# Products of the modulation grouped by four with rows turned by transposes, and sample states loaded one half ahead, in a two-layer hybrid decoder step

## The chip, the cores and the metric

The kernel runs on one core of a Trainium2 chip. The metric is the time of one launch on the device in microseconds (us), as the median of three runs. The core has five engines that work side by side, each through its own queue in order: PE (TensorE, matmuls; its weight loads are listed apart as PEld), DVE (VectorE), ACT (ScalarE), POOL (GpSimd) and SP (SyncE, which here issues most of the loads from device memory). On-chip data lies in SBUF; PE writes to PSUM, from which DVE and ACT read.

## What is computed

Two consecutive layers of a decoder, for one prompt of 512 tokens and eight sample sequences of four tokens each, which share the weights. The kernel keeps all 544 tokens as columns and the 1024 features as rows in eight tiles of 128. The two places that matter here:

```
mod = (jax.nn.silu(c) @ lw['w_ada'] + lw['b_ada'])[:, None, :]
sh1, sc1, g1, sh2, sc2, g2 = jnp.split(mod, 6, axis=-1)
h = _rmsnorm(x, lw['norm1']) * (1 + sc1) + sh1
...
def step(h, inp):
    s, d = inp
    return h * d[..., None, None] + s, h
...
y_off = jnp.einsum('bclgn,bcgrpn->bclgrp', Cm, prev) * jnp.exp(cs)[..., None]
```

The first is the modulation: nine conditioning vectors (one of the prompt, eight of the samples) times a weight of 1024 by 6144, once per layer. The second is the state-space branch: for each of eight samples and four head groups an old state of 128 by 512 is multiplied by C (the product `y_off`), decayed, added to, and written back.

## The kernel before

All large projections go through `gemm` (L325): a tile of weights (128 by 1024, 512 KB) is loaded by SP into one of four `raw` buffers, split by ACT (`wh`) and DVE (`wl`) into a high and a low part with three buffers each (`weights`, L313), and multiplied in 48 matmuls of 272 columns: eight tiles of features, three products each (high by high, high by low, low by high), two halves of the columns. Every `gemm` first calls `pump` (L136), which takes a few steps from side programs. These are Python generators in lanes; each `yield` ends a step. So the side work is laid between the gemms, step by step. A list scheduler then fixes the order of the instructions on each engine from the order of the code, priorities, its own estimate of when inputs are there, and free buffers; `high_priority(offset=WPRI)` lets weight loads run ahead. Tiles of tag "T" (49 buffers) hold most intermediates, the state tiles `h0` among them.

**The modulation** (`ada`, L235) is one side program per third of a layer's weight. Its weight comes in 16 tiles of 512 KB (`raw<-w_ada`). A tile holds two slices of the contraction; each is multiplied by `self.sc` (L253), the activated conditioning vectors padded to 32 columns, so a product takes 128 by 32 by 512 and fills 32 rows of a PSUM tile. The slice number decides which of the four row groups (0, 32, 64, 96) it goes to, so that eight slices end as four partial sums in four row groups. Between the tiles stands a `yield`. ACT copies the 128 by 512 result into `adarow`; then four matmuls (L261) with the constant `s4`, in which every 32nd row has a one in the same column, turn a 128 by 128 piece and add its four row groups. DVE adds the bias into `mod` (L262). One such block of four tiles is gone through four times per third of a layer: 24 blocks and 192 products in all. The first third of layer 0 runs at the start, before any gemm, because the first norm needs it; the others run beside the pooling branch of layer 0 and, for layer 1, beside the FFN of layer 0.

**The sample part of the state branch** (`ssd_sample`, L1028) runs once per head group and layer, eight times in all, in two halves of four samples. Per half POOL spreads B over the samples (`bbd`, L1079), SP loads four old states `h0` (L1084), a `yield` follows, then four products of 128 by 32 by 512 (L1088), one per sample and row group, into `qp`; after another `yield` there are per sample a matmul of the new input (`up`, L1100), the decay on POOL (L1103), the sum on DVE (L1106), and the store of the new state.

Of the kernel before, what the change touches and what calls it, by code (L numbers as in the profile page):

```python
# [17 lines left out]
try:  # L18
# [5 lines left out]
F32 = mybir.dt.float32  # L24
# [4 lines left out]
OP = mybir.AluOpType  # L29
AX = mybir.AxisListType  # L30
# [16 lines left out]
WPRI = 300  # L47
# [51 lines left out]
C_ID, C_CAUS, C_TRI, C_BLK, C_TRIS, C_BLKS, C_SEL, C_RW, C_HM, C_SC, C_BM, C_NM, C_RC, C_S2, C_S4 = (  # L99
    0, 128, 256, 384, 386, 418, 450, 482, 738, 746, 810, 818, 822, 886, 950)  # L100
# [3 lines left out]
class Prog:  # L104
# [130 lines left out]
    def ada(self, l, s, first=False):  # L235

        nc, a = self.nc, self.a
        par, mod, _ = self.par[l]
        m0 = 16 * s
        pick = lambda x: x.rearrange("p (h c t) n -> p c h t n", h=2, c=4)  # L240
        dst = pick(mod[:, m0:m0 + 16, :])
        bias = par[:, P_BADA + m0:P_BADA + m0 + 16].rearrange("p (h c t) -> p c h t", h=2, c=4)
        s4 = self.c[:, C_S4:C_S4 + 32]
        for c in range(4):
            ps = self.P("ada1")
            for z in range(4):
                i = 4 * c + z
                with self.tc.high_priority(offset=WPRI):
                    raw = self.wr.tile([128, 1024], F32, name="raw", tag="raw")
                    nc.sync.dma_start(raw, a["w_ada"][l, s, i])  # L250
                for q in range(2):
                    k, g = 2 * z + q, 32 * (2 * (z % 2) + q)
                    nc.tensor.matmul(ps[g:g + 32, :], self.sc[:, k, :], raw[:, q * 512:(q + 1) * 512],  # L253
                                     start=(k < 4), stop=(k >= 4))
                if z < 3:
                    yield
            row = self.t("adarow")
            self.copy("ada2", row[:, :512], ps)
            ps2 = self.P("ada2" if first else "ada3")
            for b in range(4):  # L260
                nc.tensor.matmul(ps2[:, b * 32:(b + 1) * 32], row[:, b * 128:(b + 1) * 128], s4, start=True, stop=True)  # L261
            self.E("ada1").tensor_tensor(dst[:, c], ps2[:, :128].rearrange("p (h t n) -> p h t n", h=2, t=2)[:, :, :, :9],  # L262
                                    bias[:, c, :, :, None].to_broadcast([128, 2, 2, 9]), op=OP.add)
            yield

# [762 lines left out]
    def ssd_sample(self, q):  # L1028
        nc, a, l, c = self.nc, self.a, self.l, self.c
        par = self.par[l][0]  # L1030
        csr = self.csT.bitcast(F32R)
        g, cb, Cc, xss = q["g"], q["cb"], q["C"], q["xss"]
        ps = self.P("ssd_sample1")
        for jj in range(4):
            nc.tensor.transpose(ps[:32, jj * 128:(jj + 1) * 128], xss[:, jj, :], self.ident)
# [11 lines left out]
        ps = self.P("ssd_sample2")  # L1047
# [16 lines left out]
        for jj in range(4):  # L1064
            for e in range(2):
                i = 2 * jj + e
# [8 lines left out]
        for hf in range(2):  # L1075
            bbd = self.t("bbd")
            bm = c[:32, C_BM + 4 * hf:C_BM + 4 * hf + 4, None].to_broadcast([32, 4, 128])
            for r, src in enumerate((q["bh"], q["bh"], q["bl"])):
                self.E("ssd_sample7").tensor_tensor(  # L1079
                    bbd.bitcast(F32R)[32 * r:32 * r + 32, :512].rearrange("p (b n) -> p b n", b=4),  # L1080
                    src[:, None, :].to_broadcast([32, 4, 128]), bm, op=OP.mult)
            h0s = [self.t("h0") for z in range(4)]
            for z in range(4):
                nc.sync.dma_start(h0s[z][:, :512], a["h0"][l, g, 4 * hf + z])  # L1084
            yield
            for z in range(4):
                b = 4 * hf + z
                nc.tensor.matmul(qp[32 * z:32 * z + 32, :], cm[:, 32 * b:32 * b + 32], h0s[z][:, :512],  # L1088
                                 start=(hf == 0), stop=(hf == 1))
            if hf:  # L1090
                yq = self.t("yq")
                self.copy("ssd_sample18", yq[:, :512], qp)
                for jj in range(4):
                    nc.tensor.matmul(ys[:, 128 + jj * 32:160 + jj * 32], yq[:, jj * 128:(jj + 1) * 128],
                                     c[:, C_S4:C_S4 + 32], start=True, stop=True)
            yield
            for z in range(4):
                b = 4 * hf + z
                up = self.P("ssd_sample5")
                nc.tensor.matmul(up, bbd.bitcast(F32R)[:96, z * 128:z * 128 + 128], xr[:96, :512],  # L1100
                                 start=True, stop=True)
                hn = self.t("hn0")
                self.E("ssd_sample8").tensor_tensor(hn[:, :512].rearrange("p (h d) -> p h d", h=8),  # L1103
                                        h0s[z][:, :512].rearrange("p (h d) -> p h d", h=8),
                                        self.sdec[:, b, hs, None].to_broadcast([128, 8, 64]), op=OP.mult)
                self.E("ssd_sample9").tensor_tensor(hn[:, :512], hn[:, :512], up, op=OP.add)  # L1106
                nc.scalar.dma_start(a["o_ssds"][l, g, b], hn[:, :512])
                yield
# [3 lines left out]
                                op=OP.mult)  # L1112
# [656 lines left out]
```

## Time and profile before

| What | Value |
|---|---|
| Time, median of 3 runs | 3217.64 us (3216.38 to 3218.22) |
| Time of the profiled execution | 3219.4 us |
| Its span, first to last instruction | 3217.6 us |
| PE busy | 3117.6 us, 97% |
| DVE, ACT, POOL busy | 2229.4, 1258.1, 892.9 us |
| Mean granted TensorE clock | 0.985 |
| Products L253 (modulation), busy | 92.7 us, 384 records |
| Products L1088 (old states), busy | 44.5 us, 128 records |
| Folds L261 (modulation), busy | 24.5 us, 192 records |

A matmul of 32-bit floats shows as two records in the trace, one of the split type (`wh`, `wl` with `hh`, `hl`) and one transpose as one record. Matmuls overlap in the trace, since the next begins before the last has drained; what a matmul costs the engine is therefore read from the start of one to the start of the next, not from its listed duration.

### The profile page before, as it was taken

To read this page: it belongs to the slowest core of one execution; us is meant where nothing else is said; L and a number is where in the kernel's file an instruction comes from. 1 tells how busy PE (TensorE), PEld (TensorE's weight loads), DVE (VectorE), ACT (ScalarE), POOL (GpSimd) and SP (SyncE) were. 2 spreads that over 40 slices of the span, in tenths; PEclk is the share of its full clock that TensorE was granted. 3 is DMA by queue.
4 is the path that set the end of the run, shared out by engine and by line. 5 is a ranking of instruction groups with operands and counts; after the bars stand their busy time and mean duration, and the time that the engine had idled before them with its cause. 6 is when DMAs were issued, how large, how long until landed. Compare 5 with 4: busy or idle time off the path is not lost. (4 is left out here: it accounts for less than half of the span.)

```text
span 3217.6 us, 63012 instructions
## 1 busy us (share of the span) xinstructions
PE 3117.6 (97%) x24322; PEld 2834.3 (88%) x24322; DVE 2229.4 (69%) x4827; ACT 1258.1 (39%) x2228; POOL 892.9 (28%) x1271
## 2 busy tenths in 40 slices
PE   7999999999999999999999999999999999999999
PEld 5987898999896788888989978989999967899999
DVE  5687788679878655444566877886799976564554
ACT  4344443333236534333443444433342365352432
POOL 2373445421021002111223544455120210030211
PEclk8999999999999999999999999999999999999999
DMA  6332332345433434445334323233233234333322
GB/s 231 104 104 77 110 95 101 105 151 179 164 117 129 157 133 115 147 146 147 105 104 122 98 82 106 89 96 119 95 129 117 91 125 154 106 84 94 78 98 78
DMA packets 303102, 376.85 MB, mean 117 GB/s; under 512 B 177362, under 2 KB 186930, under 8 KB 302802
## 3 DMA queue, kind: packets, MB, share of 16 engines
q1 hardware_dynamic: 116514, 315.94, 29.3%
q10 hardware_dynamic: 181216, 42.05, 6.4%
q0 software_dynamic: 5072, 14.83, 1.2%
q8 instruction: 192, 3.15, 0.4%
q14 instruction: 108, 0.88, 0.1%
HBM read 330.34 MB, written 33.79 MB: 113 GB/s over the span
## 5 line engine op out<-in xcount | busy, mean ns | idle before, releaser
L177 ACT ACTIVATE wh<-raw 128x1024 fp32r<-128x1024 f32 (+2 forms) x434 | 424.9, 980 | 1199.7 <-PE psg L336 909.6
L336 PE MATMUL psg<-hh,wh 128*128 128x272 f32 x4064 | 863.7, 292 | 7.8 <-ACT cacc L839 5.4
L336 PE MATMUL psg<-hl,wh 128*128 128x272 f32 x4064 | 856.0, 290 | 0.0
L336 PE MATMUL psg<-hh,wl 128*128 128x272 f32 x4064 | 853.6, 290 | 0.0
L322 DVE TENSOR_TENSOR wl<-raw,wh 128x1024 fp32r<-128x1024 f32 (+2 forms) x434 | 510.5, 1176 | 354.1 <-ACT wh L177 349.8
L336 PEld LDWEIGHTS psg<-hh,wh 128*128 128x128 f32 x4064 | 642.6, 189 | 61.9 <-issue 28.1
L336 PEld LDWEIGHTS psg<-hh,wl 128*128 128x128 f32 x4064 | 643.9, 189 | 17.1 <-issue 15.3
L336 PEld LDWEIGHTS psg<-hl,wh 128*128 128x128 f32 x4064 | 644.1, 189 | 15.9 <-issue 14.4
L841 POOL COPY sti<-cu 128x32 f32<-128x32 f32 x136 | 91.3, 672 | 588.9 <-ACT cu L177 588.6
L846 DVE SCALAR_TENSOR_TENSOR cacc<-cu,half,cacc 128x511 f32<-128x511 f32 x144 | 134.9, 937 | 6.8 <-ACT cacc L839 6.3
L336 PE MATMUL psg<-fh,wh 128*128 128x272 f32 x648 | 135.4, 291 | 2.6 <-DVE resid L460 2.6
L855 ACT ACTIVATE th<-cacc 128x544 f32<-128x544 f32 x92 | 60.5, 657 | 196.1 <-DVE cacc L849 187.5
L454 DVE SCALAR_TENSOR_TENSOR x<-psg,mod,x 128x272 f32<-128x272 f32 x64 | 32.0, 500 | 151.6 <-PE psg L336 142.6
L336 PE MATMUL psg<-fl,wh 128*128 128x272 f32 x648 | 133.7, 287 | 0.0
L336 PE MATMUL psg<-fh,wl 128*128 128x272 f32 x648 | 133.7, 288 | 0.0
L336 PEld LDWEIGHTS psg<-fh,wh 128*128 128x128 f32 x648 | 101.2, 188 | 14.3 <-issue 6.7
L336 PE MATMUL psg<-oh,wh 128*128 128x272 f32 x512 | 110.4, 294 | 0.0
L336 PE MATMUL psg<-ol,wh 128*128 128x272 f32 x512 | 109.5, 291 | 0.0
L336 PE MATMUL psg<-oh,wl 128*128 128x272 f32 x512 | 109.0, 292 | 0.0
L856 DVE SCALAR_TENSOR_TENSOR cacc<-th,cacc 128x544 f32<-128x544 f32 x92 | 71.3, 775 | 49.2 <-ACT th L855 49.0
L986 POOL TENSOR_TENSOR seg<-seg,cb 128x512 f32<-128x512 f32 x64 | 88.9, 1392 | 54.3 <-ACT seg L985 46.8
L336 PEld LDWEIGHTS psg<-fl,wh 128*128 128x128 f32 x648 | 101.7, 188 | 0.0
(469 smaller groups left out, 6232.4 us busy)
## 6 DMA issues: line engine op xcount, KB each, us to landing
raw<-wk SPq DMA_DIRECT2D x326, 512.0 KB, 3.5
raw<-w_ada SPq DMA_DIRECT2D x96, 512.0 KB, 3.5
h<-h SPq DMA_DIRECT2D x64, 256.0 KB, 3.8
raw<-wk SPq DMA_DIRECT2D x64, 256.0 KB, 2.8
o_ssds<-hn ACTq DMA_DIRECT2D x64, 256.0 KB, 2.2
raw<-wd SPq DMA_DIRECT2D x32, 448.0 KB, 3.4
kvr<-ckv SPq DMA_DIRECT2D x48, 256.0 KB, 3.6
kvw<-ckv SPq DMA_DIRECT2D x48, 256.0 KB, 4.0
```

The source lines that it names most:

```text
L177: self.nc.scalar.activation(out, src, AF.Copy)
L322: self.last_wl = self.E("weights1").tensor_tensor(wl[:, :n], raw[:, :n], wh[:, :n].bitcast(F32), op=OP.subtract).ins
L336: nc.tensor.matmul(o[:, c, :HC], w[:, k * 128:(k + 1) * 128], x[:, c * HC:(c + 1) * HC], start=(k == 0 and first), stop=(k == K - 1 and last))
L454: self.E("resid1").scalar_tensor_tensor(x[:, :HC], o[:, 0, :HC], g[:, 0:1], x[:, :HC], op0=OP.mult, op1=OP.add)
L841: self.E("conv1").tensor_copy(st[:, i, :, W - 1:], new)
L846: self.E("conv3").scalar_tensor_tensor(acc[:, s:512], u[:, :512 - s], wc, acc[:, s:512], op0=OP.mult, op1=OP.add)
L855: nc.scalar.activation(th, acc, AF.Tanh)
L856: self.E("silu21").scalar_tensor_tensor(acc, th, 1.0, acc, op0=OP.add, op1=OP.mult)
L986: self.E("ssd_chain5").tensor_tensor(d[:, :512], d[:, :512], cb[:, :512], op=OP.mult)
```

## The change

In `ada` the two tiles of a pair are loaded in two steps as before, but no product is issued until both are there; then four products go out one after the other, into the four row groups. The number of steps per block (four) stays. The fold by matmuls with `s4` becomes four transposes by the identity, each 128 by 128, which fill a whole PSUM tile; DVE then adds the four row groups with one reduction (`adat`), and the bias is added from there. In `ssd_sample` the four loads of the first half move to the start of the side program, those of the second half directly behind the products of the first, and the `yield` that stood between loads and products goes (two steps fewer per call).

```diff
         for c in range(4):
             ps = self.P("ada1")
-            for z in range(4):
-                i = 4 * c + z
-                with self.tc.high_priority(offset=WPRI):
-                    raw = self.wr.tile([128, 1024], F32, name="raw", tag="raw")
-                    nc.sync.dma_start(raw, a["w_ada"][l, s, i])
-                for q in range(2):
-                    k, g = 2 * z + q, 32 * (2 * (z % 2) + q)
-                    nc.tensor.matmul(ps[g:g + 32, :], self.sc[:, k, :], raw[:, q * 512:(q + 1) * 512],
-                                     start=(k < 4), stop=(k >= 4))
-                if z < 3:
+            for pair in range(2):
+                raws = []
+                for z in (2 * pair, 2 * pair + 1):
+                    with self.tc.high_priority(offset=WPRI):
+                        raw = self.wr.tile([128, 1024], F32, name="raw", tag="raw")
+                        nc.sync.dma_start(raw, a["w_ada"][l, s, 4 * c + z])
+                    raws.append(raw)
+                    if z % 2 == 0:
+                        yield
+
+                for k4 in range(4):
+                    nc.tensor.matmul(ps[32 * k4:32 * k4 + 32, :], self.sc[:, 4 * pair + k4, :],
+                                     raws[k4 // 2][:, (k4 % 2) * 512:(k4 % 2) * 512 + 512],
+                                     start=(pair == 0), stop=(pair == 1))
+                if pair == 0:
                     yield
             row = self.t("adarow")
             self.copy("ada2", row[:, :512], ps)
             ps2 = self.P("ada2" if first else "ada3")
             for b in range(4):
-                nc.tensor.matmul(ps2[:, b * 32:(b + 1) * 32], row[:, b * 128:(b + 1) * 128], s4, start=True, stop=True)
-            self.E("ada1").tensor_tensor(dst[:, c], ps2[:, :128].rearrange("p (h t n) -> p h t n", h=2, t=2)[:, :, :, :9],
+                nc.tensor.transpose(ps2[:, b * 128:(b + 1) * 128], row[:, b * 128:(b + 1) * 128], self.ident)
+
+            tot = self.s([128, 4, 9], "adat")
+            nc.vector.tensor_reduce(tot, ps2.rearrange("p (b g n) -> p b n g", b=4, g=4)[:, :, :9, :],
+                                    axis=AX.X, op=OP.add)
+            self.E("ada1").tensor_tensor(dst[:, c], tot.rearrange("p (h t) n -> p h t n", h=2),
                                     bias[:, c, :, :, None].to_broadcast([128, 2, 2, 9]), op=OP.add)
             yield
...
+        def states(hf):
+            h0s = [self.t("h0") for z in range(4)]
+            for z in range(4):
+                nc.sync.dma_start(h0s[z][:, :512], a["h0"][l, g, 4 * hf + z])
+            return h0s
+        nxt = states(0)
         ps = self.P("ssd_sample1")
...
-            h0s = [self.t("h0") for z in range(4)]
-            for z in range(4):
-                nc.sync.dma_start(h0s[z][:, :512], a["h0"][l, g, 4 * hf + z])
-            yield
+            h0s = nxt
             for z in range(4):
                 b = 4 * hf + z
                 nc.tensor.matmul(qp[32 * z:32 * z + 32, :], cm[:, 32 * b:32 * b + 32], h0s[z][:, :512],
                                  start=(hf == 0), stop=(hf == 1))
-            if hf:
+            if not hf:
+                nxt = states(1)
+            else:
                 yq = self.t("yq")
```

The diff alone doesn't tell what order the scheduler makes of it. Line numbers of the changed kernel lie some lines further down: L253 becomes L256, L261 becomes L265, L336 becomes L344, L1088 becomes L1100, L1100 becomes L1114, L1084 becomes L1045.

On PE, beside the pooling branch of layer 0, the order before has a pair of modulation products between two gemms (`psg` is a gemm's result, `raw` the modulation's weight tile, `sc` the conditioning vectors; x2 counts equal instructions in a row):

```order
L336 MATMUL psg<-hl,wh 128x272 x2
L336 MATMUL psg<-hh,wl 128x272 x2
L253 MATMUL psb<-raw,sc 32x512 x2
L336 MATMUL psg<-ph,wh 128x272 x2
L336 MATMUL psg<-pl,wh 128x272 x2
```

and the changed order, in the same part of the program, has four:

```order
L344 MATMUL psg<-hh,wl 128x272 x2
L256 MATMUL psb<-raw,sc 32x512 x4
L344 MATMUL psg<-ph,wh 128x272 x2
L344 MATMUL psg<-pl,wh 128x272 x2
```

Twice as many products now stand in one place, and the next gemm boundary has none.

On PE, in the sample part of the first head group of layer 0, the second half's products stood one by one between gemm matmuls before (`h_2731` to `h_2734` are that half's states, `cm` is C, `rel` belongs to the indexer):

```order
L1088 MATMUL psa<-h_2731,cm 32x512
L745 MATMUL psb<-rel,wsel 32x512
L336 MATMUL psg<-hh,wl 128x272 x2
L1088 MATMUL psa<-h_2732,cm 32x512
L336 MATMUL psg<-hh,wh 128x272 x2
L336 MATMUL psg<-hl,wh 128x272 x2
L336 MATMUL psg<-hh,wl 128x272
L1088 MATMUL psa<-h_2733,cm 32x512
```

Now the two halves stand close together, the second one as four in a row (`h_2492` to `h_2495` first half, `h_2631` to `h_2634` second half; `bbd` feeds the matmul of the new input, `kx` the indexer):

```order
L1100 MATMUL psa<-h_2492,cm 32x512
L1082 MATMUL psb<-smt,sxdt 64x32 x8
L1100 MATMUL psa<-h_2493,cm 32x512
L1100 MATMUL psa<-h_2494,cm 32x512
L1100 MATMUL psa<-h_2495,cm 32x512
L1114 MATMUL psb<-sxst,bbd 128x512
L748 MATMUL psa<-kx,qis 32x512 x4
L1100 MATMUL psa<-h_2631,cm 32x512
L1100 MATMUL psa<-h_2632,cm 32x512
L1100 MATMUL psa<-h_2633,cm 32x512
L1100 MATMUL psa<-h_2634,cm 32x512
```

The gemm matmuls that parted them have moved behind them, and the first matmul with `bbd` stands directly behind the first half's products.

On SP, for the same place, three weight loads lay between the first and the second half's states before:

```order
L318 DMA raw<-wk 128x1024 x2
L318 DMA raw<-wk 128x512
L1084 DMA h_2731<-h 128x512
L1084 DMA h_2732<-h 128x512
L1084 DMA h_2733<-h 128x512
L1084 DMA h_2734<-h 128x512
```

and now one, with reads of the page table (`pt`) behind it:

```order
L326 DMA raw<-wk 128x1024
L835 TENSOR_LOAD pt
L835 ISA x2
L835 TENSOR_LOAD pt
L835 ISA x2
L1045 DMA h_2631<-h 128x512
L1045 DMA h_2632<-h 128x512
```

The second half's loads stand behind one weight load instead of three.

## Rows read from the trace of the kernel before

**Rows 1.** The page's head and part 1: span; busy time, share, instructions of each engine.
```profile
span 3217.6 us, 63012 instructions
...
PE 3117.6 (97%) x24322; PEld 2834.3 (88%) x24322; DVE 2229.4 (69%) x4827; ACT 1258.1 (39%) x2228; POOL 892.9 (28%) x1271
```

**Rows 2.** Waits of PE: engine and line waited for, us in total, times, longest.
```profile
PE psa L424 <- DVE sqb L395: 14.1, 1, 14.1
PE psa L433 <- DVE rstdh L276: 10.8, 6, 3.8
PE psg L353 <- ACT hh L177: 9.0, 4, 2.5
PE psb L1100 <- DVE hn L1106: 6.3, 2, 3.4
```

**Rows 3.** Timeline of PE (start, duration, engine, line, tiles): a pair of modulation products.
```profile
660.80 0.42 PE L336 MATMUL psg<-ol,wh 128*128 128x272 f32 x2
661.06 0.41 PE L336 MATMUL psg<-oh,wl 128*128 128x272 f32 x2
661.40 1.05 PE L253 MATMUL psb<-raw,sc 128*32 128x512 f32 x4
662.38 0.52 PE L336 MATMUL psg<-oh,wh 128*128 128x272 f32 x2
```

**Rows 4.** Timeline of PE: four modulation products in a row.
```profile
717.43 0.41 PE L1213 MATMUL psg<-ph,wl 128*128 128x272 f32 x2
717.77 1.07 PE L253 MATMUL psb<-raw,sc 128*32 128x512 f32 x8
718.77 0.52 PE L1213 MATMUL psg<-ph,wh 128*128 128x272 f32 x2
```

**Rows 5.** Timeline of PE: one product of an old state alone.
```profile
227.90 0.28 PE L336 MATMUL psg<-hh,wl 128*128 128x272 f32 x1
228.12 1.04 PE L1088 MATMUL psa<-h,cm 128*32 128x512 f32 x2
229.09 0.39 PE L336 MATMUL psg<-hh,wl 128*128 128x272 f32 x1
```

**Rows 6.** Timeline of PE: the fold of a modulation block by four matmuls.
```profile
1550.73 0.29 PE L336 MATMUL psg<-hh,wl 128*128 128x272 f32 x1
1550.86 0.97 PE L261 MATMUL psb<-cst,adarow 128*128 128x32 f32 x8
1551.67 0.37 PE L336 MATMUL psg<-hh,wl 128*128 128x272 f32 x1
```

**Rows 7.** Timeline of PE: four transposes of 128 by 128.
```profile
452.31 0.41 PE L336 MATMUL psg<-hh,wl 128*128 128x272 f32 x2
452.56 0.60 PE L965 MATMUL psa<-cst,cacc 128*128 128x128 f32 x4
452.92 0.50 PE L336 MATMUL psg<-hh,wh 128*128 128x272 f32 x2
```

**Rows 8.** Windows view of 452.50 to 453.50 us (PEclk is the granted clock); all transposes of L965.
```profile
452.50:453.50 1.00, 1.00 (x10) 1.00 (x9) 1.00 (x6) 0.94 (x1) 1.00 (x1) 1.00 0.00 0
...
L965 PE MATMUL psa<-cst,cacc x128: 270/272/472, 147.3 to 2202.3; 128*128 128x128 f32 x128
```

**Rows 9.** Windows view of the first 60 us: busy PE, PEld, DVE, ACT, POOL; granted clock, DMA.
```profile
0.00:60.00 60.00, 40.04 (x204) 24.26 (x204) 28.64 (x91) 25.20 (x54) 14.72 (x45) 0.89 0.74 259
```

**Rows 10.** Groups of DVE: the bias sum and the two nearest reductions.
```profile
L1470 DVE TENSOR_REDUCE smx<-psg 128x1 f32<-128x512 f32 x16 | 11.0, 688 | 9.2 <-PE psg L1462 9.1
...
L262 DVE TENSOR_TENSOR mod<-psb,par 128x36 f32<-128x36 f32 x24 | 4.6, 190 | 35.6 <-PE psb L261 35.6
...
L1471 DVE TENSOR_REDUCE smx<-psg 64x1 f32<-64x4 f32 x16 | 2.3, 143 | 0.0
```

**Rows 11.** What the products of the old states (L1088) waited for, us and times.
```profile
  POOL cm L1072: 5.7, 4
  issue: 3.6, 18
```

**Rows 12.** Waits of SP's DMA queue, us in total, times, longest.
```profile
SPq L318 <- DVE wl L322: 1546.5, 316, 12.1
SPq L250 <- PE psb L253: 271.4, 61, 6.6
```

More of the change, by code (lines that the diff above doesn't have):

```diff
@@ L242, in ada @@
         bias = par[:, P_BADA + m0:P_BADA + m0 + 16].rearrange("p (h c t) -> p c h t", h=2, c=4)
-        s4 = self.c[:, C_S4:C_S4 + 32]
         for c in range(4):
             ps = self.P("ada1")
-            for z in range(4):
-                i = 4 * c + z
-                with self.tc.high_priority(offset=WPRI):
-                    raw = self.wr.tile([128, 1024], F32, name="raw", tag="raw")
-                    nc.sync.dma_start(raw, a["w_ada"][l, s, i])
-                for q in range(2):
-                    k, g = 2 * z + q, 32 * (2 * (z % 2) + q)
-                    nc.tensor.matmul(ps[g:g + 32, :], self.sc[:, k, :], raw[:, q * 512:(q + 1) * 512],
-                                     start=(k < 4), stop=(k >= 4))
-                if z < 3:
+            for pair in range(2):
[12 more added lines that the diff above has]
+                if pair == 0:
                     yield
```

## The prediction

> **What bounds the kernel now.** I read the page's head first: PE is busy 3117.6 us of a span of 3217.6 [rows 1], and no other engine comes near. The waits of PE say what the missing 100 us are: the longest is the wait of 14.1 us for the first norm at the start, the next are norms of later stages, 9 to 11 us each in sum, and a matmul of the sample part with 6.3 us [rows 2]. No wait on a load is among the four longest. So from about 60 us on, what PE has to issue sets the time, and the right question is what the change takes from PE's queue; what lies on DVE, ACT, POOL and SP counts only where PE would wait for it. The first 60 us differ: PE is busy 40.0 of them, at a mean granted clock of 0.89 between the two levels of 1.2 and 2.4 GHz, with the DMA engines busy 0.74 [rows 9].
>
> **What a piece costs PE.** Matmuls overlap, so I take the time from the start of one gemm row to the start of the next gemm row behind the piece, and subtract what the gemm matmuls themselves take: a row of two starts 0.25 us after the one before, 0.125 each [rows 3].
> A pair of modulation products: from 661.06 to 662.38 is 1.32, less two gemm matmuls, 1.07 us [rows 3].
> Four in a row (four row groups): 717.43 to 718.77 is 1.34, less 0.25, 1.09 us [rows 4]. So four cost what two cost; products of 32 rows each in different row groups run at the same time, and the kernel before already does this in a few places.
> One product of an old state alone: 227.90 to 229.09 is 1.19, less 0.125, 1.07 us [rows 5]. It has the same shape, so one costs as much as four.
> I call each such visit a slot, at 1.07 us. The sum is then a count of slots in the two orders.
>
> **The change, part by part.**
> *Modulation products.* The order before has 192 products in 80 runs; the first 32, in 9 runs, belong to the start. The other 71 runs hold 72 slots (one run of six has two). The changed order has 51 runs; 6 hold the first 32 products, and each of the other 45 is one slot, nearly all of them four products. 72 less 45 is 27 slots, 27 x 1.07 = 28.9 us.
> *Old states.* 64 products stood in 40 runs (30 of one, 6 of three, 4 of four), each one slot; now in 20 runs, of which two hold seven products, so 22 slots. 18 x 1.07 = 19.3 us. The load ahead hides no wait that the trace has: these products waited 5.7 us for POOL's `cm` and for no load among the listed reasons [rows 11]. The gain comes from the order alone: the scheduler took the second half's states for late and spread their products over the gemms; now it sees them early.
> *Fold.* The old one takes from 1550.73 to 1551.67, less 0.125, 0.81 us [rows 6]; four transposes of the same operands' size take from 452.31 to 452.92, less 0.25, 0.36 us [rows 7]. 20 of the 24 folds lie behind the start: 20 x 0.45 = 9.0 us.
> *The start.* Here 15 slots become 10 and four folds shorten, but PE idles a third of the time [rows 9], because norm, loads and products take turns. Ends: none of it counts, or all of it, 5 slots and 4 x 0.45, some 7 us; a loss of a few us if the loads of a pair arrive late. I take 2 us, near the lower end, since an idle engine gains little from less work.
> *DVE.* 24 reductions of 36 sums over 4 are new. No row has this shape; the nearest are 0.143 us for 64 by 4 elements and 0.688 us for 128 by 512 [rows 10]. With 144 elements per row I put it at 0.3 us, nearer the small one; 7 us in all on an engine that is busy 69% [rows 1], and the last reader, `mod`, is due a whole stage later except at the start, where 4 x 0.3 is inside the 2 us taken. Cover gone, it would cost 24 x 0.69 = 17 us at most. The bias sum stays at 0.19 us.
> *Loads.* Their number and size stay. On SP the old states move ahead of two weight loads, and the two `yield`s that went let the side program end two steps earlier per call. SP is anyway held by buffers, 1546.5 us for `raw` buffers that DVE has not released [rows 12], that is, it runs as far ahead as buffers let it; four loads more in front delay no weight that PE is about to need.
> *A new wait.* The first matmul with `bbd` now stands directly behind the first half's products. On POOL, `bbd` comes before the copy of `cm`, and the products need `cm`, so it is there. I cost it at nothing; if it is late, the price is below.
> Sum: 28.9 + 19.3 + 9.0 + 2 = 59 us. Against the profiled execution of 3219.4 us that is 3160; the median of the runs lies 1.8 us lower at 3217.64, so I predict 3158 us.
>
> **A rule against the transposes.** Rows of transposes show 0.09 us each, at a granted clock of 1.00, the 2.4 GHz level, in the stretch around them [rows 7, 8]. The Trainium skill, page "TensorE: Matmul & The Clock Gate", section "Part 4: PE-mode transpose", puts a transpose at about 275 ns inside a kernel and says that it doesn't count as activity for the clock gate as a matmul does. By that figure a fold would take 1.1 us instead of 0.81, an estimate by that page, and the folds would cost 6 us instead of giving 9, which makes the sum 3173. The row speaks against it, so the sum goes by the row.
>
> **The rivals.**
> *A, the sample part gives its gain back.* With 18 slots fewer, PE reaches the matmuls of the new input sooner, and these wait for POOL and DVE, as they already do: 6.3 us in two waits, the longest 3.4 [rows 2]. If each of the 16 halves waits 1.2 us more, the 19.3 us are gone, and the time is 3158 + 19 = 3177. For it: the waits exist. Against: the gemms beside the products can fill in, and the waits are few. 14%.
> *B, transposes slow PE.* If the four didn't overlap and each took the longest duration of such a transpose, 0.472 us [rows 8], a fold would take 1.89 us, 1.08 more than the old one; 20 x (1.08 + 0.45) = 31 us off the forecast, 3189 us. Against it: the median is 0.272 and four take 0.36. By the skill's rule named above this is the case in which the clock drops around them. 3%.
> *C, slower: weights come late.* A modulation tile of even number now keeps one of four `raw` buffers until its partner's turn, a gemm later, 48 x 0.125 = 6.0 us; SP already waits 271.4 us in 61 waits for these products to free buffers [rows 12], and the gemms' weights stand behind in the same queue. From 59/45 = 1.3 us of late weights per group of four on, the kernel is slower than before; at 2 us it would be 3158 + 90 = 3248. Against: three split weights in front of PE are some 18 us of cover, and no wait on split weights is among PE's longest [rows 2]. 6%.
> *D, four don't run as four.* If products whose two tiles come from different loads went as two pairs, the 45 slots behind the start would stay 72, and only the other terms count: 3217.64 - 30 = 3187. Against: the row of four [rows 4] took two tiles as well. 5%.
>
> **How the numbers follow.** The forecast itself, a gain of 45 to 75 us, gets the remaining 72%; the predicted time is its middle, 3158. Its upper end of gain takes the whole start and the waits of 5.7 us for `cm`, some 70 us, and a little for waits that go with fewer interruptions; its lower end takes the DVE or half of rival A. The range for 8 in 10 is 3143 to 3182: 75 us of gain below, and above it the forecast's own edge and most of A; B, C, D and a part of A stay outside. A measurement of this kernel can tell 0.2%, 6.4 us, from no change. Faster by more than that: forecast, A, B, D, together 94%; no difference 1% and slower 5%, both from C, which has either end.
>
> **What would show it.** In the profile after: rows of eight records of modulation products where rows of four stood, each about 1.07 to 1.09 us between gemm rows; products of old states in eights, 20 rows of them; rows of four transposes at 0.36 us; PE's busy time down by some 55 to 60 us to about 3060, its idle time still near 100 us; DVE's busy time up by about 7 us. Wrong would be: idle time of PE grown by 20 us or more with waits on `hn`, `bbd` or split weights (A, C); a lower granted clock around the transposes (B); eights that last 2 us (D).

## The result and the profile after

| | Before | After |
|---|---|---|
| Median of 4 runs | 3217.93 us (3216.38 to 3227.65) | 3169.76 us (3166.91 to 3172.43) |
| Ratio, with its 95% interval | | 0.9844 (0.9825 to 0.9862) |
| Profiled execution, span | 3217.6 us | 3165.1 us |
| PE busy; idle (span less busy) | 3117.6; 100.0 us | 3057.6; 107.5 us |
| Mean granted clock | 0.985 | 0.984 |

The kernel became faster by 50 us (44 to 56 by the interval, times 3218). The predicted 3158 was 12 us too low, and 3169.76 lies within the range of 3143 to 3182.

The page's head after, which answers to [rows 1]:

```profile
span 3165.1 us, 62821 instructions
...
PE 3057.6 (97%) x24226; PEld 2817.8 (89%) x24226; DVE 2225.3 (70%) x4851; ACT 1258.7 (40%) x2228; POOL 888.7 (28%) x1271
```

PE lost 60.0 us of work, a little more than the 59 that were counted, but the span fell by 52.5: 7.5 us came back as idle time. So the first question is where PE idles now. Its waits after (total, times, longest), beside [rows 2]:

```profile
PE psa L432 <- DVE sqb L403: 14.1, 1, 14.1
PE psg L361 <- ACT hh L177: 12.3, 5, 3.5
PE psa L441 <- DVE rstdh L284: 10.8, 6, 3.8
PE psa L973 <- DVE cb L961: 8.0, 2, 4.0
PE psg L344 <- DVE ol L318: 6.9, 4, 2.1
PE psg L344 <- DVE zt L910: 4.7, 4, 1.3
...
PE psb L1114 <- DVE hn L1120: 2.6, 3, 1.2
```

The waits on `cb`, `ol` and `zt` make 19.6 us, all three in the state branch; before, only 2.8 us for `cb` were on the list. `cb` is a head group's masked product of B and C (`ssd_prep`), `ol` the low part of a head group's normed output, input of its out projection, and `zt` a gate. Other waits of the state branch have shrunk or gone: `hn`, at which rival A looked, from 6.3 to 2.6, `cacc` from 5.4 to 1.7, and `wks` with 5.3 is off the list. So the growth of 7.5 us is the difference between new waits and old ones.

Now the pieces themselves, in the timeline of PE. Four modulation products (answers to [rows 3, 4]), four products of old states [rows 5] and a fold [rows 6]:

```profile
714.40 0.41 PE L1227 MATMUL psg<-ph,wl 128*128 128x272 f32 x2
714.75 1.07 PE L256 MATMUL psb<-raw,sc 128*32 128x512 f32 x8
715.74 0.52 PE L1227 MATMUL psg<-ph,wh 128*128 128x272 f32 x2
...
356.34 0.29 PE L344 MATMUL psg<-hh,wh 128*128 128x272 f32 x1
356.56 1.07 PE L1100 MATMUL psa<-h,cm 128*32 128x512 f32 x8
357.55 0.50 PE L791 MATMUL psa<-ikh,qs 128*128 128x512 f32 x1
...
840.07 0.29 PE L344 MATMUL psg<-ph,wh 128*128 128x272 f32 x1
840.20 0.60 PE L265 MATMUL psb<-cst,adarow 128*128 128x128 f32 x4
840.56 0.37 PE L344 MATMUL psg<-ph,wh 128*128 128x272 f32 x1
```

Read as in the prediction, start to start less the gemm matmuls of 0.125 each: 1.34 - 0.25 = 1.09 us for four modulation products, 1.21 - 0.125 = 1.09 for four states, 0.49 - 0.125 = 0.36 for a fold. All three prices are those of the prediction. The first 60 us, beside [rows 9], and DVE's two groups of the modulation, beside [rows 10]:

```profile
0.00:60.00 60.00, 36.09 (x191) 20.84 (x192) 29.27 (x95) 25.11 (x54) 13.22 (x45) 0.89 0.77 260
...
L268 DVE TENSOR_REDUCE adat<-psb 128x36 f32<-128x144 f32 x24 | 7.2, 299 | 12.0 <-PE psb L265 12.0
...
L270 DVE TENSOR_TENSOR mod<-adat,par 128x36 f32<-128x36 f32 x24 | 4.9, 202 | 0.4
```

PE does 4 us less at the start (40.04 before), but waits as much more there: within these 60 us the wait on `hh` goes from 2.5 to 5.9 us and the one on the modulation's weight from 1.6 to 3.2, and the 480th gemm matmul starts only 0.2 us sooner. This is one execution: in the eight kernels below whose modulation and fold are both those of the change, that matmul starts between 2.0 us later and 4.5 us sooner than before. The reduction takes 299 ns. DVE's busy time in all fell by 4.1 us all the same, 2229.4 to 2225.3.

Where the gain arises is read from three places that both programs pass: the first matmul of a norm's broadcast at the end of layer 0's mixers, at the end of its FFN, and at the end of layer 1's mixers. Before, and then after:

```profile
1198.14 1.03 PE L433 MATMUL psa<-cst,rstdh 128*128 128x128 f32 x6 [1.84 <-DVE rstdh L276]
...
1672.42 0.80 PE L433 MATMUL psa<-cst,rstdh 128*128 128x128 f32 x2 [3.81 <-DVE rstdh L276]
...
2801.42 0.80 PE L433 MATMUL psa<-cst,rstdh 128*128 128x128 f32 x2 [3.61 <-DVE rstdh L276]
```

```profile
1180.07 1.03 PE L441 MATMUL psa<-cst,rstdh 128*128 128x128 f32 x6 [1.84 <-DVE rstdh L284]
...
1631.08 1.22 PE L441 MATMUL psa<-cst,rstdh 128*128 128x128 f32 x4 [3.81 <-DVE rstdh L284]
...
2749.01 1.24 PE L441 MATMUL psa<-cst,rstdh 128*128 128x128 f32 x6 [3.61 <-DVE rstdh L284]
```

Layer 0's mixers gain 18.1 us, its FFN 41.3 - 18.1 = 23.2, layer 1's mixers 52.4 - 41.3 = 11.1. The FFN holds modulation alone (three fifths of what lies behind the start, by the counts 3/5 x 37.9 = 22.7), and there the count is met. Layer 0's mixers hold the other two fifths, 15.2, and half of the old states, 9.7: 24.9 counted, 18.1 came; modulation alone (below) leads by 14.9 us at that place, so what is missing there is the states' part. Layer 1's mixers hold the other half of the old states, 9.7, and there 11.1 came, although the program and its new waits are the same in both layers. The windows view of these stretches parts it into work and idle time. Behind the first 60 us PE's busy time falls by 20.3 us in layer 0's mixers (1113.2 to 1092.9) and its idle time grows by 2.2; in layer 1's mixers PE's busy time falls by 12.7 us (1093.7 to 1081.0) and its idle time grows by 1.6. Part of the difference is the granted clock, as the last section shows: a stretch at the low level that is new in layer 0 was there already before in layer 1. A single pair of traces thus sizes the gap only to some us.

### The profile page after: what moved, and what is told of

The parts are those of the page before. It is cut to its first block, busy times and chain, and to the rows that moved or that the text cites. A ratio compares the mean times of both kernels' runs of the same rounds, so it can differ in the third digit from the quotient of the medians.

```text
span 3165.1 us, 62821 instructions
## 1 busy us (share of the span) xinstructions
PE 3057.6 (97%) x24226; PEld 2817.8 (89%) x24226; DVE 2225.3 (70%) x4851; ACT 1258.7 (40%) x2228; POOL 888.7 (28%) x1271
## 4 chain that ended last, share of the span: by engine, by line
PE 78%; DVE 8%; issue 4%; POOL 3%; DMA 3%; ACT 3%; ACTq 1%; SPq 0%; POOLq 0%; DVEq 0%
PE psg L344 60%; PE psg L361 2%; DMA raw<-wk 2%; PE psb L256 1%; DVE wl L330 1%; POOL hn L1117 1%; PE psb L1014 1%; PE psb L1411 1%; PE psb L1000 1%; PE psa L567 1%; ACT wh L177 1%; PE psa L1406 1%; POOL bbd L1094 1%; PE psb L1023 1%; ACTq L1578 1%
## 5 line engine op out<-in xcount | busy, mean ns | idle before, releaser
L344 PE MATMUL psg<-hh,wh 128*128 128x272 f32 x4064 | 857.0, 290 | 7.8 <-DVE zt L910 4.7
L344 PE MATMUL psg<-hl,wh 128*128 128x272 f32 x4064 | 853.5, 290 | 0.0
L344 PE MATMUL psg<-hh,wl 128*128 128x272 f32 x4064 | 848.9, 289 | 0.0
L344 PEld LDWEIGHTS psg<-hh,wh 128*128 128x128 f32 x4064 | 642.0, 189 | 40.5 <-issue 21.0
L344 PEld LDWEIGHTS psg<-hh,wl 128*128 128x128 f32 x4064 | 641.9, 189 | 8.9 <-issue 7.3
L344 PEld LDWEIGHTS psg<-hl,wh 128*128 128x128 f32 x4064 | 641.8, 189 | 6.4 <-issue 4.5
L849 POOL COPY sti<-cu 128x32 f32<-128x32 f32 x136 | 84.2, 619 | 526.9 <-ACT cu L177 519.9
L344 PE MATMUL psg<-fh,wh 128*128 128x272 f32 x648 | 134.9, 290 | 2.6 <-DVE resid L468 2.6
L344 PE MATMUL psg<-fl,wh 128*128 128x272 f32 x648 | 134.1, 288 | 0.0
L344 PE MATMUL psg<-fh,wl 128*128 128x272 f32 x648 | 133.9, 288 | 0.0
L344 PE MATMUL psg<-ol,wh 128*128 128x272 f32 x512 | 110.7, 293 | 6.9 <-DVE ol L318 6.9
L344 PE MATMUL psg<-oh,wh 128*128 128x272 f32 x512 | 110.7, 296 | 0.8 <-ACT oh L177 0.8
L344 PEld LDWEIGHTS psg<-fh,wh 128*128 128x128 f32 x648 | 101.2, 188 | 10.9 <-issue 5.0
L344 PE MATMUL psg<-oh,wl 128*128 128x272 f32 x512 | 110.2, 292 | 0.0
L1588 POOL TENSOR_TENSOR cacc<-cacc 128x544 f32<-128x544 f32 x44 | 62.9, 1429 | 159.8 <-DVE cacc L864 159.8
L344 PEld LDWEIGHTS psg<-fl,wh 128*128 128x128 f32 x648 | 101.8, 188 | 0.8 <-issue 0.8
```

What stands on the lines that cost most here:

```text
L344: nc.tensor.matmul(o[:, c, :HC], w[:, k * 128:(k + 1) * 128], x[:, c * HC:(c + 1) * HC], start=(k == 0 and first), stop=(k == K - 1 and last))
L849: self.E("conv1").tensor_copy(st[:, i, :, W - 1:], new)
L1588: self.E("ffn3").tensor_tensor(s_, s_, aa, op=OP.mult)
```

## The experiments

Three theories were put against each other at first: that the modulation part gives all that was counted and the states about half (theory 1); that the states give all and the modulation less; and, within theory 1, several mechanisms for the half that is missing (1a to 1d, told with the runs). Gains below are 3218 times one less the ratio to the kernel before.

**Modulation alone** (the sample part as before):

```diff
-        nxt = states(0)
...
-            h0s = nxt
+            h0s = [self.t("h0") for z in range(4)]
+            for z in range(4):
+                nc.sync.dma_start(h0s[z][:, :512], a["h0"][l, g, 4 * hf + z])
+            yield
```

> Only the modulation part of the change (fours and transposes); the sample part is as before. Theory 1 (the count is right, and what is missing of 59 us was given back in the sample part): 28.9 + 9.0 us gained, 36 to 40, all between 590 and 1600 us of the span, nothing at the start. Theory 2 (the modulation part is short of its count, because weight buffers are held longer): a gain under 30 us, with waits of PE on split weights.

Measured: 3183.29 us, ratio 0.9881 (0.9865 to 0.9898), a gain of 38 us (33 to 43). The count says 28.9 + 9.0 = 37.9. The modulation gives what it was counted at. Its profile shows no growth of idle time (98.9 us).

**Old states alone** (`ada` as before):

> Only the states loaded ahead and the step taken out; the modulation is as before. Theory 1: the products of the old states cost PE 20 us less, but waits of PE in the state branch grow and leave a gain of 8 to 14 us in all. Theory 2: the whole 19 us arrive.

Measured: 3212.69 us, 0.9973 (0.9962 to 0.9984), 8.7 us (5 to 12) where 19.3 were counted. Theory 1 holds. In its profile PE's busy time falls by 16.7 us (3117.6 to 3100.9) and its idle time grows by 11.2 (100.0 to 111.2), with the same two new waits as in the change:

```profile
PE psa L965 <- DVE cb L953: 8.0, 2, 4.0
PE psg L336 <- DVE ol L310: 6.4, 4, 2.1
```

**The dropped step kept, loads ahead**, and **the step dropped, loads in place**, to part the two halves of the edit to the sample part:

```diff
             h0s = nxt
+            yield
             for z in range(4):
```

> The change with one line more: the step between the loads and the products of the old states stays. Theory 1a (the missing step draws later work of the state branch forward, so that PE meets it before POOL and DVE are ready): the added waits go, the products stay in fours, and the gain is 55 to 60 us, 3158 to 3163. Theory 1b (the waits come from the products standing close together, whatever the number of steps): the time stays within 3 us of the change, 3167 to 3173.

```diff
-            h0s = nxt
+            h0s = [self.t("h0") for z in range(4)]
+            for z in range(4):
+                nc.sync.dma_start(h0s[z][:, :512], a["h0"][l, g, 4 * hf + z])
             for z in range(4):
```

> The change with the loads of the old states in their old place, but without the step behind them. Products of old states stand alone again (42 runs). Theory 1a: the gain of the states is lost and the added waits stay, so that 36 to 40 us of the modulation less 6 to 10 us of waits remain, 3184 to 3190. Theory 1b: the modulation's gain alone, 36 to 40 us, 3178 to 3182.

Measured: 3181.30 (0.9880, 0.9864 to 0.9895) with the step kept, where PE's order has the states in 21 runs, and 3186.01 (0.9890, 0.9872 to 0.9907) with the loads in place, where it has 42. The second was as 1a expected: the loads ahead are what brings the states together. The first missed both forecasts by 8 us and more: with the loads ahead and the step kept, the states' gain is gone although they stand together; PE's idle time is 116.7 us. Neither 1a nor 1b says why.

**Fours with the old fold** (the sample part as before, the fold by matmuls with `s4`) and **the new fold alone** (all else as before):

```diff
-                nc.tensor.transpose(ps2[:, b * 128:(b + 1) * 128], row[:, b * 128:(b + 1) * 128], self.ident)
...
+                nc.tensor.matmul(ps2[:, b * 32:(b + 1) * 32], row[:, b * 128:(b + 1) * 128], s4, start=True, stop=True)
```

> Only the products of the modulation in fours; the fold by matmuls and the sample part are as before. Theory 1 (slots by count): 28.9 us less 1 or 2 for the start, 27 to 29 us gained, each four at 1.21 us from the gemm matmul before to the one behind. Rival (fours from two loads run as two pairs): no gain, fours at 1.9 us or more.

> Only the fold by transposes and a reduction; products and the sample part are as before. Theory 1: 20 x 0.45 = 9 us less a few waits for the copy of the rows, 6 to 9 us gained, PE's granted clock unchanged. Rival (transposes slow PE down): no gain or a loss, folds of over 0.8 us.

Measured: fours alone 3191.21, 0.9909 (0.9891 to 0.9927), 29.3 us (23 to 35) against 28.9 counted: rival D falls. The fold alone 3215.87, 0.9990 (0.9980 to 1.0), 3.2 us (0 to 6.4), less than the 9.0 counted; yet modulation alone less fours alone is 38 - 29.3 = 9, with some 8 us of uncertainty, and the profiled execution of the fold alone has a span 7.4 us shorter than that of before, 5.4 of it PE's busy time. So a fold's price is known (0.36 against 0.81 us), and what 20 of them are worth in the whole is not settled between nothing and the 9 us counted.

**The wait on `cb`.** The longest new wait seemed the culprit. In the timeline of PE after, at the handover from the first head group to the second (the place where the finish of one group and the preparation of the next meet):

```profile
258.03 0.25 PE L956 MATMUL psa<-cacc 128*32 128x32 f32 x2
262.27 1.09 PE L973 MATMUL psa<-cst,cacc 128*128 128x128 f32 x4 [4.00 <-DVE cb L961]
```

The transposes of L973 need one of two PSUM buffers, which DVE frees only when it has read `cb` from it; DVE has older work in front (the splits of `ol`), and is done at 262.2 us; in the kernel before it was done at 261.8. There PE came at about 260 and waited 1.41 us; now it comes at 258.3. Three kernels were to move this wait: the split of `ol` on POOL, so that DVE has less in front (rival: another DVE or POOL chain takes its place); `cb` in the other pair of PSUM buffers (1d); and two more steps behind the sample part (1c: the two dropped steps set how far PE runs ahead).

```diff
-        self.E("split1").tensor_tensor(lo.bitcast(F32R), src, hi, op=OP.subtract)
+        (nc.gpsimd if names == "o" else nc.vector).tensor_tensor(lo.bitcast(F32R), src, hi, op=OP.subtract)
```

> The change, with the low parts of the finished state-branch rows (four subtractions of 0.72 us per head group, queued on DVE in front of the reads that free PSUM in the next group's preparation) made on POOL. Theory 1c (PE waits there because DVE is late, with these subtractions in front): the wait of 4.0 us per layer at the transposes shrinks by 2 to 3 us, and the gain over the change is 4 to 8 us, 3162 to 3166. Rival (POOL becomes the late one, at some 1.3 us each): waits on the low parts grow, and the time is the change's or up to 10 us more.

```diff
-    "ssd_chain5", "ssd_prep1", "ssd_sample3", "ssd_sample5",)
+    "ssd_chain5", "ssd_prep1", "ssd_prep2", "ssd_sample3", "ssd_sample5",)
```

> The change, with the second PSUM tile of the state branch's preparation taken from the other pair of PSUM buffers. Theory 1d (PE waits for a free PSUM buffer, not for the data): the wait of 4.0 us per layer at the transposes goes, 4 to 8 us gained over the change, 3162 to 3166. Rival (the data themselves come late, and PE meets the same DVE work one step later): the wait moves to the next reader, and the time stays within 3 us of the change.

```diff
             for jj in range(4):
                 self.E("ssd_sample15").tensor_copy(q["Y"][jj][:, 512:], ecs[:, jj * 32:(jj + 1) * 32])
         yield
+        yield
+        yield
```

> The change, with two empty steps behind the sample part, so that the finish of a head group comes at its old distance while loads and products stay as the change has them. Theory 1c (the finish, drawn forward by the two missing steps, lies in front of the next group's preparation on DVE): the wait of 4.0 us per layer at the transposes falls below 1.5 us, and the gain over the change is 4 to 8 us. Theory 1d (PE gets there earlier than DVE can free PSUM, wherever the finish stands): the wait stays above 3 us and the time within 4 us of the change.

Measured: split on POOL 3174.13 (0.9863, 0.9846 to 0.9879), `cb` still waited for, 7.3 us, so 1c missed. The time is in the rival's range, but not by the rival's way: the waits on `ol` fell from 6.9 us to 0.6, and others grew instead, `hn` from 2.6 to 7.0 and `cacc` from 1.7 to 6.3:

```profile
PE psb L1114 <- DVE hn L1120: 7.0, 3, 5.3
PE psg L344 <- ACT cacc L847: 6.3, 4, 1.7
```

The other PSUM pair 3160.48 (0.9815, 0.9799 to 0.9832), 59.5 us of gain: a little more than 1d expected, and the best so far. Two steps behind 3180.16 (0.9880, 0.9863 to 0.9896): the wait on `cb` is gone and the time is 10 us worse, so 1c falls; 1d, which expected the wait to stay and the time within 4 us, missed too. In the waits of the kernel with two steps behind, others stand:

```profile
PE psg L344 <- ACT cacc L847: 9.4, 6, 2.2
PE psb L1114 <- DVE hn L1120: 8.6, 5, 4.5
PE psa L748 <- issue: 7.9, 2, 4.0
PE psb L1014 <- DVE wks L770: 5.3, 2, 2.6
```

Three of them are on the list of the kernel before as well (5.4, 6.3 and 5.3 us); the one of 7.9 us is new.

**Is it the wait on `cb` that the other PSUM pair saves?** The same edit on the kernel before, where PE hardly waits for `cb`, and the edit together with the two steps:

> The kernel before, with the second PSUM tile of the state branch's preparation from the other pair of buffers. Theory 1d (this wait was made by the time that the change frees on PE): little to gain here, where the wait at this place is 1.4 us per layer, 0 to 4 us. Rival (the other pair of buffers is better in any case): 7 us or more, as in the changed kernel.

> The change with both: the PSUM tile of the preparation from the other pair, and two empty steps behind the sample part. If both theories hold in part, the gains add, 3152 to 3158; if they remove the same wait, the time is that with the PSUM tile alone, 3157 to 3164.

Measured: on the kernel before 3209.14 (0.9966, 0.9951 to 0.9980), 10.9 us (6 to 16), where 1d expected 0 to 4 and the rival 7 or more; its profiled execution, with a span of 3220.0, shows no gain at all. Together 3172.38 (0.9856, 0.9838 to 0.9874), worse than either expectation: the steps cost some 12 us again. So 1d came near the number for a reason that wasn't shown, and `cb` was in doubt. The trace of the other PSUM pair speaks against `cb` too: at the first handover PE waits 4.06 us there for other tiles (1.75 for `xdt`, 2.31 for `kx`), against 4.36 in the change.

**The handovers.** Counting gemm matmuls along PE's timeline shows at which point the change loses against before. The lead swings by some us as side work moves between gemms, but one loss stays: with the gemm matmul that starts at 532 us before, the change leads by 7.8 us, at 540 us by 0.8 and at 700 us by 2.7; the kernel with the other PSUM pair leads by 7.1, 6.6 and 9.6. In that stretch lies the third handover: a head group's norm broadcast (L303), the preparation of the next group (L950 to L956), then the first group's out projection (`oh`, `ol`). Before, in the timeline of PE:

```profile
521.55 1.05 PE L295 MATMUL psa<-cst,rstd 128*128 128x128 f32 x8
...
522.87 0.40 PE L336 MATMUL psg<-hl,wh 128*128 128x272 f32 x1
...
532.99 0.41 PE L336 MATMUL psg<-oh,wh 128*128 128x272 f32 x2
533.24 0.42 PE L336 MATMUL psg<-ol,wh 128*128 128x272 f32 x2
```

and after:

```profile
525.16 1.05 PE L303 MATMUL psa<-cst,rstd 128*128 128x128 f32 x8
...
527.49 1.16 PE L950 MATMUL psa<-cacc 128*128 128x128 f32 x8 [0.94 <-ACT rb L177]
...
529.34 0.77 PE L344 MATMUL psg<-oh,wh 128*128 128x272 f32 x4 [0.40 <-ACT oh L177]
532.20 0.52 PE L344 MATMUL psg<-ol,wh 128*128 128x272 f32 x2 [2.09 <-DVE ol L318]
```

Between broadcast and out projection ACT copies the norm (`rb`), DVE multiplies four tiles by it (2.87 us for L1151), and ACT and DVE split them into `oh` and `ol`. Before, 69 records of gemm matmuls lie in between and cover this; now none. PE stands at it for 0.94 + 0.40 + 2.09 = 3.43 us, and at the second handover for 0.35 + 1.36 = 1.71. From the first state product of the group to the norm broadcast it takes 38.9 us (486.3 to 525.2), before 37.6 (483.9 to 521.5): that chain over POOL and DVE has become no shorter, while the states' products of this group stand in 2 rows instead of 6. Why the scheduler's order then leaves no gemm matmul behind the broadcast is not shown; by the table the loads and the dropped step both have a part in it. By kernel, records of gemm matmuls between broadcast and out projection in layer 0, PE's waits from the one to 6 us into the other (in layer 1 the counts differ by at most 8), and PE's idle time in the whole execution (span less busy):

| Kernel | Second handover | Third handover | PE idle in all |
|---|---|---|---|
| before | 34; 0 us | 69; 0 us | 100.0 us |
| modulation alone | 34; 0 | 69; 0 | 98.9 |
| loads in place | 56; 0 | 31; 0 | 104.2 |
| states alone | 0; 1.7 | 0; 3.0 | 111.2 |
| the change | 0; 1.7 | 0; 3.4 | 107.5 |
| the step kept | 0; 2.0 | 75; 0 | 116.7 |
| two steps behind | 0; 2.0 | 69; 0 | 113.0 |
| split on POOL | 0; 0.7 | 64; 0 | 113.0 |
| other PSUM pair | 6; 2.0 | 64; 0 | 100.9 |
| other PSUM pair and two steps | 4; 2.9 | 64; 0 | 110.0 |

In the change that is 2 x (1.71 + 3.43) = 10.3 us over the two layers, near what is missing (59 less 50), and the states alone have the same waits. The size alone proves little: the waits on `cb` and `zt` are new too, others went, and the split on POOL took most of these handover waits away (2 x 0.7 us are left) without a gain. The other PSUM pair, which was meant for `cb`, happens to give the third handover its cover back. A last kernel tests the handovers by themselves: it moves one gemm (the third gate projection) from behind the out projection to in front of it, with the same work.

```diff
                     self.flush(prev["fin"])
+                    zz(jj - 1)
                     branch(g - 1, prev["out"])
-                if jj:
+                elif jj:
                     zz(jj - 1)
```

> Edit: the change, with the gemm of the third gate projection moved from behind the out projection of the group before to ahead of it, so that it stands between that group's norm broadcast and its out projection at the second and third handover between head groups, in both layers. Same work. Theory H (the missing 10 us are the handovers: in the change no gemm matmul stands between the norm broadcast and the out projection there, and PE waits 0.35 + 1.36 us at the second and 1.34 + 2.09 us at the third handover, in both layers, 10.3 us in sum, for rb, oh and ol): these waits go, 42 and 43 records of gemm matmuls stand in between as cover, and the time is 3170 less 10, 3157 to 3163 us; PE's waits on ol fall from 6.9 us to under 1. Rival (the chain on POOL and DVE from old states to out projection sets the time of a head group, and waits only wander): the waits on ol go but as much comes back elsewhere in the state branch, 3166 to 3174 us.

The edit acts at the first handover as well, where 106 records now stand instead of 64.

Measured: 3159.09 us (3155.99 to 3167.32), 0.9818 (0.9803 to 0.9833), a gain of 58.6 us; better than the change by 10.7 us by the medians, by 8.4 by the ratios and by 7.1 by the spans of the profiled executions. The time is in the range of theory H. The same place in its timeline of PE:

```profile
523.37 1.05 PE L303 MATMUL psa<-cst,rstd 128*128 128x128 f32 x8
...
524.68 0.39 PE L344 MATMUL psg<-hh,wl 128*128 128x272 f32 x1
...
531.56 0.41 PE L344 MATMUL psg<-oh,wh 128*128 128x272 f32 x2
531.81 0.41 PE L344 MATMUL psg<-ol,wh 128*128 128x272 f32 x2
```

and the head of its page, with the rows for `cb` and `zt` of its waits of PE, in which `ol` does not appear any more:

```profile
span 3158.0 us, 62827 instructions
...
PE 3057.5 (97%) x24226; PEld 2818.0 (89%) x24226; DVE 2225.1 (70%) x4851; ACT 1257.7 (40%) x2228; POOL 888.8 (28%) x1271
...
PE psa L974 <- DVE cb L962: 9.5, 2, 4.7
PE psg L344 <- DVE zt L910: 5.3, 4, 1.3
```

The waits at the third handover are gone, those at the second are down to 0.37 + 0.60 us. PE is busy for 3057.5 us, as in the change (3057.6), and its idle time falls from 107.5 to 100.5 us, that of the kernel before; in the windows view it falls by 4.7 us in layer 0's mixers and by 4.9 in layer 1's, which is near the 5.1 us per layer. And the wait on `cb` is still there, 1.5 us longer than in the change: the predicted time is reached with it. So for this order it was the handovers, not `cb`, and the rival falls. It does not fall everywhere: in the kernel with the split on POOL the handovers were covered better and as much came back as other waits. The kernel with the gemm moved and the one with the other PSUM pair are the best two, and their intervals don't part them; both beat the kernel before, and their ratios touch that of the change only at the edge (0.9833 and 0.9832 against 0.9825).

What stays open: why the kernels with more steps (kept, or behind) and the one with the split on POOL are 4 to 12 us slower than the change. Their handovers are better covered; with the steps behind, PE stands at the waits listed for that kernel instead (`hn`, `cacc`, `wks`, 7.9 us ahead of the indexer's matmul), with the split on POOL at `hn` and `cacc`, and no run takes these away one by one. So cover at the handovers is not enough by itself. Open too is the gain of the other PSUM pair, on the change as on the kernel before.

## Why the prediction was right, and what was mis-sized

*What bounds the kernel.* Right: PE busy fell by 60.0 us and the span by 52.5; DVE's and POOL's shares stayed.

*Modulation products, 28.9 us.* Right: 29.3 us measured alone (23 to 35). That four cost what two cost was read from a single place [rows 4], and it holds in the sum.

*Fold, 9.0 us.* The price was right (0.36 us). The worth in the whole came out at 3 by itself and 9 beside the fours, so the term is right or too high by an amount that these runs don't settle. The Trainium skill, page "TensorE: Matmul & The Clock Gate", section "Part 4: PE-mode transpose", puts one at about 275 ns. The trace agrees with it as the listed duration of one, 0.272 us in the median [rows 8]; but four in a row take 0.36 us from start to start, 0.09 each, so 1.1 us for four (an estimate, 4 x 0.275) is not what a row of them costs PE. The mean clock doesn't differ (0.984 after, 0.985 before). So rival B falls.

*The start, 2 us.* 0.2 us in the profiled execution, where PE had 4 us less work and waited as much more, as the prediction's reason for its lower end (an idle engine gains little) has it. The other kernels with the same start scatter from 2.0 us later to 4.5 us sooner than before, so the term is not resolved.

*DVE and loads, nothing.* Right: 24 x 299 ns = 7.2 us, estimated 7, and no wait on split weights among PE's waits, so rival C falls. The loads of the modulation at the start came later (PE's waits on them went from 1.6 to 3.2 us).

*Old states, 19.3 us.* This is the term that was mis-sized: 8.7 us alone, 50 - 38 = 12 beside the modulation. PE's work did fall as counted (start to start, the states' products of layer 0 take 10.7 us instead of 20.4). The step that failed is "A new wait", costed at nothing, which looked at one place only, the first matmul with `bbd`. Rival A had the mechanism (PE comes sooner to what POOL and DVE must finish first) and put it at the same place, 1.2 us in each of 16 halves. It came at another: 5.1 us per layer at two of the three handovers to the out projection, 10.3 in all. With a gemm put in front, the time is 3159.09, against a forecast of 3158, and PE's idle time is again the 100 us that the sum took for granted. That it comes so near is in part luck, since the start and the fold may have given less than counted, and the waits on `cb` and `zt` are still in it. That the order after has no gemm matmul there stood in the order of the change, and was not looked for.

*What would show it.* Rows of eight at 1.07, states in 20 runs (8 of them eights, the others rows of two, six and fourteen), folds at 0.36, PE busy near 3060 and DVE's reductions at 7 us all came; "idle time still near 100 us" did not: 107.5. DVE's busy time did not rise by 7 us but fell by 4.1.

## What to carry to other kernels

When work is taken from the engine that sets the time, or its order changes, cover for the slower chains can go with it. List what is issued between each producer's last step on the slow chain and its first reader, before and after: where the count falls to nothing, price the chain's length there as a wait. The longest new wait was not the one to mend here: compare the lead at points that both programs pass, and look in the stretch where it is lost. Then watch the idle time of the whole, since a wait that is taken away at one place can come back at another, as with the split on POOL.

## What was not expected of the hardware

At the 4.0-us wait on `cb` the granted clock falls, and stays low behind it. In the windows view (length, busy PE, PEld, DVE, ACT, POOL, granted clock, DMA share, GB/s), the work ahead of the wait, the wait and the work behind it:

```profile
256.00:258.30 2.30, 2.28 (x20) 1.95 (x19) 2.30 (x5) 1.83 (x3) 0.00 (x0) 1.00 0.43 143
258.30:262.30 4.00, 0.03 (x1) 0.06 (x1) 3.93 (x8) 1.84 (x4) 0.00 (x0) 0.88 0.12 36
262.30:272.00 9.70, 9.32 (x32) 4.14 (x32) 3.81 (x12) 3.00 (x6) 3.58 (x3) 0.52 0.13 41
```

PE is busy 9.32 of the 9.70 us behind the wait at 0.52, near the 1.2 GHz level, where four transposes of L973 take 0.74 us (262.27 to 263.01) instead of the 0.36 of [rows 7]. It would be easy to put this down to the length of the wait. The kernel before speaks against that: at the same place PE waits 1.41 us for `cb` in both layers, and behind it the clock is 1.00 in layer 0 and low in layer 1:

```profile
261.56:271.30 9.74, 7.59 (x36) 3.14 (x36) 5.50 (x19) 3.28 (x7) 2.68 (x3) 1.00 0.17 51
...
1892.10 1.46 PE L740 MATMUL psa<-kx,qis 64*32 64x512 f32 x6 [1.41 <-DVE cb L943]
...
1892.25:1902.00 9.75, 8.73 (x24) 3.79 (x22) 3.87 (x12) 1.22 (x3) 1.05 (x1) 0.56 0.17 52
```

So the same instructions behind the same wait ran at either level in one execution. The low stretch costs PE more than the wait alone: if all of the 9.32 us scaled with the clock, they would be 4.8 us at 1.00, an estimate. In layer 0 it is new with the change, in layer 1 it isn't, which is part of why the two layers gained differently in these traces. The kernel with the gemm moved has the wait of 4.7 us and a low stretch behind it too, and is among the fastest; so the clock does not explain what was missing.
